# Layer A's weight sums stored ahead, one 1/rms by matmuls, and earlier splits of the second half's activations

## The chip, the cores and the metric

The kernel runs on one core of a Trainium2 chip (trn2). The metric is the time of one execution on the device in microseconds (us). A core has five engines that work side by side, each in its own order: PE (TensorE, the matmuls; PEld is its weight load), DVE (VectorE), ACT (ScalarE), POOL (GpSimd) and SP (SyncE, which here issues the DMA transfers). They wait for one another by semaphores. A DMA can also be issued on POOL's own queue.

## The reference

Two layers over x (2048 tokens of 1024), each `x <- x + mixer(RMSNorm(x))`, then a last RMSNorm. Layer A is a gated linear recurrence, layer B a short gated convolution; the width inside is 1536.

```python
def rmsnorm(x, g):
    inv = lax.rsqrt(jnp.mean(xf * xf, axis=-1, keepdims=True) + NORM_EPS)
    return xf * inv * g
def recurrent_mixer(h, ...):              # layer A
    u = einsum('bsd,dc->bsc', h, w_in)    # in-projection, 1024 -> 2 x 1536
    gate, xb = u[..., :WIDTH], u[..., WIDTH:]
    y = rg_lru(causal_depthwise_conv(xb, conv_w, conv_b), gate_w, gate_b, lam)
    return einsum('bsc,cd->bsd', y * silu(gate), w_out)   # out-projection, 1536 -> 1024
def shortconv_mixer(h, ...):              # layer B: in-projection to 4 x 1536
    return einsum('bsc,cd->bsd', bg * conv(cg * xv) * silu(gate), w_out)
```

## The kernel before

The kernel is one function, `trunk`. It works in four stages: layer A's in-projection (`in_A`, to about 646 us), layer A's out-projection (`OutSums.run`, about 646 to 868 us), layer B's in-projection and layer B's out-projection. Tokens are cut into four chunks of 512 (c = 0 to 3), two to a half. The instructions of each engine stand in an order that the framework's scheduler fixes when the kernel is built; an engine runs them strictly in that order.

**Precision.** A float32 matrix product is made of float16 parts. `split_out` (l. 1113) and `split_w` (l. 1186) make from a float32 tile a pair of float16 tiles: ACT writes the rounded value, DVE the remainder. `mm3` (l. 495) then issues three matmuls. A tile that ends up as a weight pair is called `wf`, `wv` or (on its way to DRAM) `wy`; one of the activations z is called `zs`.

**The out-projection** uses seven products instead of eight for each 2 x 2 block multiplication (Strassen and Winograd). The weights' blocks A11, A12, A21, A22 give S1 = A21 + A22, S2 = S1 - A11, S3 = A11 - A21 and S4 = A12 - S2; the activations' blocks z give T1 to T4 likewise. `ORDERS` names the seven pairs for the first half of the tokens and for the second. Each pair has four products (q = 0 to 3), so n runs from 0 to 27 in the first half and from 28 to 55 in the second. A product is 18 matmuls: KH = 6 blocks k of the inner dimension by three. After it DVE adds its result to x in `add_to_x` (l. 1300), one product late.

What a product needs is fetched and split by two lists with due times in units of n: `fetch` (SP's loads `load_z`, `load_w`, `load_raw`, `load_x`) and `splits` (`split_z`, `make_w`). The weight pairs A11, S2, S3, A22 and A12 stay in `wf` for both halves; S1 and S4 are read twice. Before the change only S1 and S4 come ready from DRAM: they were made in the in-projection by `weights` (l. 1195), a generator that loads the four raw blocks of one k, lets POOL add them (`combinations`, l. 476 to 492, the sums being l. 481), splits them and stores them. The five that stay are made in the out-projection by `make_w`: raw blocks `wo` are loaded, POOL makes S2 (two sums) and S3 (one) in l. 1233, and ACT and DVE split them (l. 1188 and 1189).

**What runs beside the in-projection.** `extra` holds generators that `advance` (l. 653) steps at each of some 188 stages of `in_A`. An entry is [counter, pace, generator]; at each stage the counter rises by one, and

```python
            if e[0] % e[1] == 0 and next(e[2], "end") == "end":
```

decides whether the generator takes a step. `weights` begins with `out_scale` (l. 810 on), which loads all 24 raw blocks and squares them on ACT (l. 816), and then goes on with the six k. Elsewhere ACT works on the recurrence in the same stretch: the gates' `tg` (tanh of the PSUM tile `pg`, l. 908), `a`, the square root of l. 926, which needs another function table (ACT_TABLE_LOAD), the squares `junk` of the next weights (l. 379) and their splits `wc` (l. 417). `pg` has two buffers, so PE's gate matmuls (l. 904) wait when ACT is late with `tg`.

**1/rms of layer A's result.** `emitA` adds the squares of each finished row block: ACT squares (l. 226), POOL adds to `sa` (l. 227). When a chunk is done, `endA` defers two steps of `inv_between` (l. 289) by so many products: the sum over partitions by four tiny matmuls (l. 233), then Sqrt on ACT (l. 245), a reciprocal on DVE (l. 246) and the spreading of the 512 values over all partitions. The spreading is done in two ways. With a queue (chunk 1 only, on POOL's): a write `rd<-r` to DRAM of 512 values of 4 bytes (l. 249) and a read back that repeats them for every partition, `inv<-rd` (l. 250). Without one: DVE makes four diagonal tiles `dg` (l. 256), PE multiplies them by ones (l. 259), ACT copies (l. 262). Chunk 1 ends before chunk 0 in the first half.

Of the kernel before, what the change touches and what calls it, by code (L numbers as in the profile page):

```python
# [11 lines left out]
ALU = mybir.AluOpType  # L12
# [20 lines left out]
KH = NH // 2  # L33
# [13 lines left out]
def trunk(ctx, tc, xT, xn, prm, wa, ga, oa, wb, ob, out):  # L47
# [18 lines left out]
    }  # L66
    wt = {
        (l, n, k): dr.tile([P, 2, CH], F16, name=f"w{l}{n}_{k}", tag=f"w{l}{n}_{k}")
        for l, names in (("A", ("S1", "S4")), ("B", ("A11", "A12", "A22", "S1", "S2", "S3", "S4")))
        for n in names  # L70
        for k in range(NH // 2)
    }
# [578 lines left out]
    extra = []  # L651
# [479 lines left out]
        "A12": ("B21", (0, 0), True),  # L1131
    }

    NZS = 18

    class OutSums:

# [9 lines left out]
        STAY = ("A11", "S2", "S3", "A22", "A12")  # L1147
        PREPARED = 2 * KH

        RAW = {"A11": (0,), "A12": (1,), "A22": (3,), "S3": (0, 2), "S2": (2, 3, 0)}  # L1150

        def __init__(self, l, wdram, wsc):
            self.l, self.wdram, self.wsc = l, wdram, wsc
# [2 lines left out]
            for half, order in enumerate(self.ORDERS):  # L1156
                seen = set()
                for p, name in enumerate(order):
                    n = 28 * half + 4 * p - (2 if l == "B" and half and p == 6 else 0)
                    for k in range(KH):  # L1160
                        at = n - 6 + 2 * k / 3
                        splits.append((at, self.split_z, half, name, k))
                        fetch.append((at - 3, self.load_z, half, name, k))
                        if half and name in self.STAY:
                            continue
                        if l == "B" or name not in self.STAY:
                            fetch.append((n - 5 + k / 100, self.load_w, half, name, k))
                            continue
                        splits.append((at + 0.1, self.make_w, name, k))
                        for r in self.RAW[name]:  # L1170
                            fetch.append((at - 2.9, self.load_raw, name, k, r))
                    dest = SEVEN[name][1]
                    if dest not in seen:
                        seen.add(dest)
                        for q in range(ND):
                            fetch.append((n + q - 3, self.load_x, half, dest, q))
# [18 lines left out]
        def weights(self, pre):  # L1195

            yield from pre
            for k in range(KH):
# [5 lines left out]
                for name, a in combinations(raw):  # L1204
                    if (self.l, name, k) in wt:
                        sp.dma_start(wt[self.l, name, k], self.split_w(wk, "wy", 2, a))
                        yield
                    if self.l == "A" and name == "S4":
                        break

        def load_z(self, half, name, k):
# [8 lines left out]
            self.wops[name, k] = t  # L1220
            return sp.dma_start(t, wt[self.l, name, k])

        def load_raw(self, name, k, n):
            t = self.raw[name, k, n] = buf(wp, "wo", "wo", 10)
            return sp.dma_start(t, self.raw_w(k, n))

        def make_w(self, name, k):
            raw = [self.raw.pop((name, k, n)) for n in self.RAW[name]]
            a = raw[0]
            for n, b in enumerate(raw[1:]):  # L1230
                t = buf(wp, "ws", "ws", 2)
                add = name == "S2" and n == 0
                g.tensor_tensor(out=t, in0=a, in1=b, op=ALU.add if add else ALU.subtract)
                a = t
            self.wops[name, k] = self.split_w(wp, "wf", 5 * KH, a)

        def load_x(self, half, dest, q):
            m, c = dest
# [196 lines left out]
            run(extra.pop(0)[2])  # L1435

    outA, startA = follows("A", oa, wsc[0])
    extra.append([-24, 3, outA.weights(preA)])
    in_A(hA, w0, head, sideA, startA, nothing)
    while sideA:  # L1440
        advance(sideA)
# [18 lines left out]
    def endA(c, ts):  # L1460
        if c == 3:
            return
        steps = inv_between(sums[c], inv[c // 2][c % 2], g if c == 1 else None)
        for n in (2, 3):
            defer(lambda: next(steps, None), n)

    def besideA(n):
# [241 lines left out]
```

## Time and profile before

| | us |
|---|---|
| median of 3 runs | 1993.2 |
| lowest, highest | 1989.6, 1994.15 |
| profiled execution, its own time | 1994.0 |
| its span, first to last instruction | 1992.2 |
| PE busy | 1943.2 (98%) |
| DVE, ACT, POOL busy | 1276.9, 1100.8, 728.0 |

The span's mean granted TensorE clock is 0.988. The profile is of one execution; a view of its trace gives start times from the span's start. In a timeline row stand start, duration, engine, line, operation, output and inputs, shape and count; what stands in brackets at its end is how long the engine was idle before it, and whose work ended that. Consecutive instructions of one kind can share a row. Matmuls overlap, so the distance of two starts, not the duration, says what one costs. The granted clock has two levels, full (2.4 GHz, 1.00) and half (1.2 GHz).

### The profile page before, as it was taken

What the parts mean: (1) busy time and instruction counts of PE and PEld (TensorE: products, weight loads), DVE (VectorE), ACT (ScalarE), POOL (GpSimd) and SP (SyncE); (2) the same over time, 40 slices, a digit from 0 to 9 for tenths busy, and PEclk for the clock granted to TensorE, in tenths of its full rate; (3) what the DMA queues carried; (4) which work ended last, traced back from release to release, by engine and by line L of the source; (5) the groups of instructions that cost most, each with busy time, mean ns of one, the idle gap of its engine ahead of it and who ended that gap; (6) DMA issues with size and microseconds to landing.
All of it is one profiled execution on the core that took longest, in us unless ns stands there. A gap on an engine that the chain in (4) does not pass through costs nothing.

```text
span 1992.2 us, 25454 instructions
## 1 busy us (share of the span) xinstructions
PE 1943.2 (98%) x8922; PEld 905.2 (45%) x8922; DVE 1276.9 (64%) x2094; ACT 1100.8 (55%) x1967; POOL 728.0 (37%) x568
## 2 busy tenths in 40 slices
PE   7999999999999998989999999999999999999998
PEld 3444444444444444444444444444444444444447
DVE  8977677767577696979635755746636336544465
ACT  7878867776667563545644443544443452544442
POOL 0012324230303360343552673664553453522321
PEclk9999999999999998999999999999999999999999
DMA  9223334220206987531241241242130030395662
GB/s 322 88 85 95 107 100 137 80 96 32 90 1 223 389 291 226 166 111 53 75 143 38 85 164 43 90 148 69 64 111 28 23 120 27 120 360 194 171 223 85
DMA packets 155617, 252.71 MB, mean 127 GB/s; under 512 B 15392, under 2 KB 52896, under 8 KB 155488
## 3 DMA queue, kind: packets, MB, share of 16 engines
q1 hardware_dynamic: 155152, 250.29, 37.3%
q8 instruction: 70, 1.15, 0.2%
q0 software_dynamic: 336, 0.79, 0.1%
q14 instruction: 59, 0.48, 0.1%
HBM read 176.04 MB, written 74.98 MB: 126 GB/s over the span
## 4 chain that ended last, share of the span: by engine, by line
PE 80%; issue 7%; DVE 6%; ACT 3%; DMA 2%; POOL 1%; DVEq 0%; POOLq 0%; ACTq 0%; SPq 0%
PE acc L497 12%; PE acc L501 12%; PE acc L500 12%; PE p L501 8%; PE p L497 8%; PE p L500 8%; PE r L497 4%; PE r L500 4%; PE r L501 4%; PE pg L904 2%; PE q L500 2%; PE q L501 2%; PE q L497 2%; DVE u L930 1%; DVE op L310 1%
## 5 line engine op out<-in xcount | busy, mean ns | idle before, releaser
L497 PEld LDWEIGHTS <-wc 128*128 128x128 f16 x2096 | 208.3, 99 | 262.4 <-issue 21.2
L500 PEld LDWEIGHTS <-wc 128*128 128x128 f16 x2096 | 205.7, 98 | 261.3 <-issue 28.0
L501 PEld LDWEIGHTS <-wc 128*128 128x128 f16 x2096 | 205.7, 98 | 260.1 <-issue 19.3
L497 PE MATMUL acc<-op,wc 128*128 128x512 f16 x752 | 285.0, 381 | 9.8 <-DVE u L871 3.3
L497 PE MATMUL p<-op,wc 128*128 128x512 f16 x768 | 291.5, 380 | 1.4 <-ACT wc L417 1.2
L500 PE MATMUL p<-op,wc 128*128 128x512 f16 x768 | 291.8, 380 | 0.0
L501 PE MATMUL p<-op,wc 128*128 128x512 f16 x768 | 291.2, 380 | 0.4 <-DVE wc L418 0.4
L500 PE MATMUL acc<-op,wc 128*128 128x512 f16 x752 | 286.8, 382 | 2.2 <-DVE op L310 2.2
L501 PE MATMUL acc<-op,wc 128*128 128x512 f16 x752 | 287.4, 382 | 0.0
L929 POOL TENSOR_TENSOR u<-fixed,u 128x512 f32<-128x512 f32 x48 | 52.2, 1109 | 361.3 <-ACT fixed L926 359.5
L418 DVE SCALAR_TENSOR_TENSOR wc<-ws,fixed,wc 128x512 f16<-128x512 f32 x104 | 105.1, 1015 | 82.1 <-ACT wc L417 72.1
L418 DVE SCALAR_TENSOR_TENSOR wc<-wr,fixed,wc 128x512 f16<-128x512 f32 x122 | 106.7, 893 | 77.7 <-ACT wc L417 72.4
L227 POOL TENSOR_TENSOR sa<-sa,sq 128x512 f32<-128x512 f32 x48 | 74.6, 1554 | 202.9 <-ACT sq L226 199.9
L1300 DVE SCALAR_TENSOR_TENSOR xo<-acc,fixed,xo 128x512 f32<-128x512 f32 (+1 forms) x120 | 84.6, 709 | 99.0 <-PE acc L501 98.6
L501 PE MATMUL r<-op,wc 128*128 128x512 f16 x384 | 145.5, 379 | 0.0
L500 PE MATMUL r<-op,wc 128*128 128x512 f16 x384 | 145.5, 379 | 0.0
L497 PE MATMUL r<-op,wc 128*128 128x512 f16 x384 | 145.5, 379 | 0.0
L993 POOL TENSOR_TENSOR pb<-pb,cg 128x512 f32<-128x512 f32 x48 | 68.8, 1433 | 187.5 <-DVE fixed L391 99.2
L862 DVE SCALAR_TENSOR_TENSOR u<-acc,fixed,u 128x511 f32<-128x511 f32 (+2 forms) x138 | 100.9, 742 | 51.5 <-ACT u L860 51.5
L417 ACT ACTIVATE wc<-wr,fixed 128x512 f16<-128x512 f32 x122 | 83.6, 711 | 78.7 <-DVE fixed L394 77.1
L904 PE MATMUL pg<-u,gts 128*128 128x512 f32 x192 | 98.7, 607 | 3.9 <-ACT tg L908 3.9
L481 POOL TENSOR_TENSOR ws<-wr 128x512 f32<-128x512 f32 x52 | 78.1, 1503 | 59.1 <-DVE wc L418 29.3
(213 smaller groups left out, 3932.8 us busy)
## 6 DMA issues: line engine op xcount, KB each, us to landing
wr<-in_wb SPq DMA_DIRECT2D x104, 256.0 KB, 3.2
zAT<-u SPq DMA_DIRECT2D x48, 256.0 KB, 2.2
zr<-zAT SPq DMA_DIRECT2D x48, 256.0 KB, 5.1
wo<-in_oa SPq DMA_DIRECT2D x48, 256.0 KB, 5.3
zr<-zBT SPq DMA_DIRECT2D x48, 256.0 KB, 5.3
wr<-in_wa SPq DMA_DIRECT2D x44, 256.0 KB, 3.8
zAB<-sg SPq DMA_DIRECT2D x36, 256.0 KB, 2.0
zr<-zAB SPq DMA_DIRECT2D x36, 256.0 KB, 5.3
```

The lines of the kernel that those rows point to most:

```text
L227: squared[0] = eng.tensor_tensor(out=acc, in0=acc, in1=sq, op=ALU.add)
L417: last_hi[0] = s.activation(t[:, 0, :], src, AF.Copy, scale=sw[:, 2:3])
L418: v.scalar_tensor_tensor(out=t[:, 1, :], in0=src, scalar=sw[:, 2:3], in1=t[:, 0, :], op0=ALU.mult, op1=ALU.subtract,)
L481: g.tensor_tensor(out=t, in0=x, in1=y, op=op)
L497: ins = nc.tensor.matmul(acc, wh, xh, start=start, stop=False, **kw)
L500: nc.tensor.matmul(acc, wh, xl, start=False, stop=False, **kw)
L501: return nc.tensor.matmul(acc, wl, xh, start=False, stop=stop, **kw)
L862: v.scalar_tensor_tensor(out=u[:, n:], in0=a[:, 0 : CH - n], scalar=ac(3 - n), in1=u[:, n:], op0=ALU.mult, op1=ALU.add,)
L904: ins = nc.tensor.matmul(pg, gw[m][:, oo], u, start=True, stop=True)
L929: g.tensor_tensor(out=u, in0=w, in1=u, op=ALU.mult)
L993: g.tensor_tensor(out=t, in0=t, in1=cg[m, half, c], op=ALU.mult)
L1300: ins = v.scalar_tensor_tensor(out=x[:, ts], in0=acc[:, ts], scalar=zsc[half][:, 2:3], in1=x[:, ts], op0=ALU.mult, op1=ALU.add,)
```

## The change

It has four parts.

1. S2 and S3 of layer A are stored in DRAM too. `weights` for A goes on to S3 in the order S1, S2, S4, S3: twelve more splits `wy`, six more sums (S3; S2 is needed for S4 already) and twelve more stores in the in-projection. In the out-projection `load_w` fetches S2 and S3 into `wf`, twelve loads in the place of thirty raw ones; `make_w` is left with A11, A12 and A22, and l. 1233 with its eighteen sums is gone. `wo` has 6 buffers instead of 10.
2. The splits of the second half's z are due at 16 + (6p + k) * 2/3 (16 to 43.3) instead of 22 + 4p + 2k/3 (22 to 49.3), their loads three earlier, with 30 buffers `zs` instead of 18.
3. The entry of `weights` in `extra` is [-60, 2] instead of [-24, 3].
4. Chunk 1's 1/rms is spread by matmuls like the others', and the second step of `inv_between` is deferred by 4 products instead of 3 for all three chunks.

```diff
-        for l, names in (("A", ("S1", "S4")), ("B", ("A11", "A12", "A22", "S1", "S2", "S3", "S4")))
+        for l, names in (("A", ("S1", "S2", "S3", "S4")), ("B", ("A11", "A12", "A22", "S1", "S2", "S3", "S4")))
...
-    NZS = 18
+    NZS = 30
...
-        RAW = {"A11": (0,), "A12": (1,), "A22": (3,), "S3": (0, 2), "S2": (2, 3, 0)}
+        RAW = {"A11": 0, "A12": 1, "A22": 3}
...
                         at = n - 6 + 2 * k / 3
+                        if l == "A" and half:
+                            at = 16 + (KH * p + k) * 2 / 3
                         splits.append((at, self.split_z, half, name, k))
                         fetch.append((at - 3, self.load_z, half, name, k))
                         if half and name in self.STAY:
                             continue
-                        if l == "B" or name not in self.STAY:
+                        if (l, name, k) in wt:
                             fetch.append((n - 5 + k / 100, self.load_w, half, name, k))
                             continue
                         splits.append((at + 0.1, self.make_w, name, k))
-                        for r in self.RAW[name]:
-                            fetch.append((at - 2.9, self.load_raw, name, k, r))
+                        fetch.append((at - 2.9, self.load_raw, name, k))
...
-                    if self.l == "A" and name == "S4":
+                    if self.l == "A" and name == "S3":
                         break
...
-        def load_raw(self, name, k, n):
-            t = self.raw[name, k, n] = buf(wp, "wo", "wo", 10)
-            return sp.dma_start(t, self.raw_w(k, n))
+        def load_raw(self, name, k):
+            t = self.raw[name, k] = buf(wp, "wo", "wo", 6)
+            return sp.dma_start(t, self.raw_w(k, self.RAW[name]))
 
         def make_w(self, name, k):
-            raw = [self.raw.pop((name, k, n)) for n in self.RAW[name]]
-            a = raw[0]
-            for n, b in enumerate(raw[1:]):
-                t = buf(wp, "ws", "ws", 2)
-                add = name == "S2" and n == 0
-                g.tensor_tensor(out=t, in0=a, in1=b, op=ALU.add if add else ALU.subtract)
-                a = t
-            self.wops[name, k] = self.split_w(wp, "wf", 5 * KH, a)
+            self.wops[name, k] = self.split_w(wp, "wf", 5 * KH, self.raw.pop((name, k)))
...
-    extra.append([-24, 3, outA.weights(preA)])
+    extra.append([-60, 2, outA.weights(preA)])
...
-        steps = inv_between(sums[c], inv[c // 2][c % 2], g if c == 1 else None)
-        for n in (2, 3):
+        steps = inv_between(sums[c], inv[c // 2][c % 2])
+        for n in (2, 4):
             defer(lambda: next(steps, None), n)
```

POOL at the end of the first half, before (`ws<-wo` are the sums of l. 1233, `sa` the squares of the chunks):

```order
L1233 TENSOR_TENSOR ws<-wo 128x512 x5
L227 TENSOR_TENSOR sa<-sa,sq 128x512
L1233 TENSOR_TENSOR ws<-wo 128x512
L227 TENSOR_TENSOR sa<-sa,sq 128x512 x8
L249 DMA rd<-r 128x4x1
L250 DMA inv<-rd 128x512
L227 TENSOR_TENSOR sa<-sa,sq 128x512 x5
L481 TENSOR_TENSOR ws<-wr 128x512
```

POOL at the same place, with the change:

```order
L764 TENSOR_TENSOR u<-sg,u 128x512
L227 TENSOR_TENSOR sa<-sa,sq 128x512 x17
L481 TENSOR_TENSOR ws<-wr 128x512
L481 TENSOR_TENSOR ws<-ws,wr 128x512
L227 TENSOR_TENSOR sa<-sa,sq 128x512 x2
```

The sums and the two DMAs have left the queue, and the squares stand in one run.

ACT in the in-projection, the stretch that the trace of before shows from 212.60 us on (the square root, the splits `wc` of the next weights, the two `tg` of a gate), before:

```order
L926 ACT_TABLE_LOAD
L926 ACTIVATE fixed<-fixed 128x1024
L417 ACTIVATE wc<-wr,fixed 128x512 x4
L908 ACT_TABLE_LOAD
L908 ACTIVATE tg_2012<-pg,fixed 128x512
L379 ACTIVATE junk,fixed<-wr 128x512 x2
L908 ACTIVATE tg_2016<-pg,fixed 128x512
```

ACT at the same place, with the change:

```order
L926 ACT_TABLE_LOAD
L926 ACTIVATE fixed<-fixed 128x1024
L1189 ACTIVATE wy<-ws,fixed 128x512 x2
L379 ACTIVATE junk,fixed<-wr 128x512
L417 ACTIVATE wc<-wr,fixed 128x512 x4
L1189 ACTIVATE wy<-ws,fixed 128x512
L908 ACT_TABLE_LOAD
L908 ACTIVATE tg_2056<-pg,fixed 128x512
L1189 ACTIVATE wy<-ws,fixed 128x512
L908 ACTIVATE tg_2060<-pg,fixed 128x512
```

Three splits `wy` and one `junk` now stand between the square root and the first `tg`. (In the changed file the ACT half of `split_w` is l. 1189.)

## Rows read from the trace of the kernel before

**Rows 1.** The page: engines, busy us (share of the span), instructions.

```profile
PE 1943.2 (98%) x8922; PEld 905.2 (45%) x8922; DVE 1276.9 (64%) x2094; ACT 1100.8 (55%) x1967; POOL 728.0 (37%) x568
```

**Rows 2.** Windows: stretch, its length, busy us of each engine, PEclk, DMA share, GB/s.

```profile
50.00:240.00 190.00, 178.35 (x734) 80.14 (x734) 142.90 (x273) 157.73 (x281) 35.78 (x28) 0.96 0.29 94
240.00:640.00 400.00, 398.20 (x1731) 181.19 (x1730) 278.21 (x513) 275.65 (x440) 109.74 (x83) 1.00 0.27 90
755.00:768.00 13.00, 6.75 (x20) 3.50 (x21) 3.85 (x6) 2.89 (x4) 3.09 (x3) 0.62 0.82 240
748.00:760.00 12.00, 6.86 (x32) 2.94 (x30) 0.33 (x1) 0.63 (x1) 1.90 (x3) 0.92 0.37 29
1871.00:1881.00 10.00, 10.00 (x48) 4.55 (x47) 4.90 (x7) 0.34 (x1) 0.00 (x0) 1.00 1.06 143
```

**Rows 3.** Timeline of POOL, the small write and the read behind it.

```profile
745.74 0.92 POOL L249 DMA_DIRECT2D rd<-r  x1
758.01 0.56 POOL L250 DMA_DIRECT2D inv<-rd  x1 [11.35 <-DMA rd<-r]
```

**Rows 4.** Timeline of PE behind that, L233 and the first matmuls.

```profile
761.25 1.87 PE L233 MATMUL ss<-fixed,sa 128*128 128x1 f32 x8 [6.39 <-POOL sa L227]
762.98 0.59 PE L497 MATMUL acc<-zs,wf 128*128 128x512 f16 x1
...
768.38 0.38 PE L500 MATMUL acc<-zs,wf 128*128 128x512 f16 x1
```

**Rows 5.** Timeline of PE near 713 us.

```profile
713.18 0.38 PE L497 MATMUL acc<-zs,wf 128*128 128x512 f16 x1 [2.47 <-DVE xo L1300]
...
713.99 0.63 PE L497 MATMUL acc<-zs,wf 128*128 128x512 f16 x1
...
717.24 0.38 PE L501 MATMUL acc<-zs,wf 128*128 128x512 f16 x1
```

**Rows 6.** Source view of lines 1188 and 1189: ns of one, min/median/max.

```profile
L1188 ACT ACTIVATE wy<-ws,fixed x36: 705/712/724, 285.3 to 1430.7; 128x512 f16<-128x512 f32 x36
...
L1189 DVE SCALAR_TENSOR_TENSOR wf<-ws,fixed,wf x12: 739/1374/1755, 681.5 to 720.7; 128x512 f16<-128x512 f32 x12
```

**Rows 7.** Timeline of PE near 857 us, the 1/rms of chunk 2.

```profile
853.39 0.38 PE L497 MATMUL acc<-zs,wv 128*128 128x512 f16 x1
857.63 0.79 PE L259 MATMUL pn<-dg,fixed 128*128 128x128 f32 x2 [3.87 <-DVE dg L256]
...
861.09 0.63 PE L500 MATMUL acc<-zs,wv 128*128 128x512 f16 x1
...
863.97 0.38 PE L501 MATMUL acc<-zs,wv 128*128 128x512 f16 x1
```

**Rows 8.** Timeline of DVE: product 49's add, dg of chunks 2 and 0.

```profile
854.77 0.74 DVE L1300 SCALAR_TENSOR_TENSOR xo<-acc,fixed,xo 128x512 f32<-128x512 f32 x1
...
856.57 3.65 DVE L256 TENSOR_SCALAR dg<-fixed,r 128x128 f32<-128x128 f32 x4
...
769.82 0.87 DVE L256 TENSOR_SCALAR dg<-fixed,r 128x128 f32<-128x128 f32 x4
```

**Rows 9.** Groups by line, 640 to 755 us: count, busy us, mean ns, idle.

```profile
L1116 DVE SCALAR_TENSOR_TENSOR zs<-zr,fixed,zs 128x512 f16<-128x512 f32 x43 | 43.5, 1021 | 5.3 <-ACT zs L1115 5.1
...
L1189 DVE SCALAR_TENSOR_TENSOR wf<-ws,fixed,wf 128x512 f16<-128x512 f32 x12 | 15.0, 1253 | 3.9 <-ACT wf L1188 3.9
...
L1233 POOL TENSOR_TENSOR ws<-wo 128x512 f32<-128x512 f32 x12 | 18.4, 1543 | 37.3 <-DMA wo<-in_oa 35.2 <-DVE wf L1189 1.9 <-POOL ws L1233 0.2
```

**Rows 10.** Timeline of PE, waits in the in-projection.

```profile
125.75 0.38 PE L497 MATMUL acc<-op,wc 128*128 128x512 f16 x1 [3.33 <-DVE u L871]
...
219.45 2.07 PE L904 MATMUL pg<-u,gts 128*128 128x512 f32 x2 [3.94 <-ACT tg L908]
```

**Rows 11.** Timeline of ACT before that tg.

```profile
214.85 2.54 ACT L417 ACTIVATE wc<-wr,fixed 128x512 f16<-128x512 f32 x4
```

**Rows 12.** Source view of line 249, its three writes.

```profile
DMA to landing us min/median/max: 10.8/11.7/12.0
```

## The prediction

> **What bounds the kernel now.** I read the page first: PE is busy for 1943.2 of 1992.2 us [rows 1]. The 49 us in which it idles, and what it loses at half clock, are all that this change can win, since it removes no product. The windows view says where they lie [rows 2]: from 240 to 640 us PE is busy for 398.20 of 400.00, so nothing is to be had there; from 50 to 240 us, in layer A's in-projection, for 178.35 of 190.00; from 755 to 768 us, in its out-projection, for 6.75 of 13.00 at a clock of 0.62. About 0.2% (4 us) is what a measurement of this kernel can tell from no change.
>
> In the out-projection I then read the timelines, and three waits stand out. **Near 755 us** POOL issues the small write `rd<-r` at 745.74, and its queue stands 11.35 us until the write has landed and `inv<-rd` may go [rows 3]. Chunk 0's squares, which POOL has to add, are queued behind it, and PE's L233 waits for those: 6.39 us idle, then half clock [rows 4], with thirteen matmul starts from 762.98 to 768.38. **At 713 us** PE waits 2.47 us for DVE's add L1300 and then runs at half clock, eight starts from 713.99 to 717.24 [rows 5]. DVE is late there since it splits S2, S3 and z beside POOL's sums L1233: one such split takes between 0.74 and 1.76 us [rows 6]. **At 857 us** the matmuls L259 of chunk 2 wait 3.87 us for DVE's `dg`, and half clock follows till 863.97 [rows 7]. Behind it stands DVE's queue: product 49's add ran at 854.77 [rows 8], though PE had done with that product some 845 us in (two products of 18 matmuls and an L233 back from 853.39); the Sqrt of chunk 2 is behind that add's square in ACT's order; and the four `dg` then took 3.65 us, where chunk 0's took 0.87 [rows 8].
>
> **The change, part by part.** The sum is made against the profiled execution's own time, 1994.0 us; the median of the three runs, 1993.2, is 0.8 lower. Where PE ran at half clock, 1.2 instead of 2.4 GHz, half of the time is counted as lost.
>
> **A, 1/rms of chunk 1 by matmuls.** `rd<-r` and `inv<-rd` leave POOL's queue, and chunk 0's squares (17 in a row now) have nothing before them. Gone are 6.39 us idle, half of L233's 1.87, and half of the 5.40 us of thirteen starts [rows 4]: 6.4 + 0.9 + 2.7 = 10.0. New on PE are four L259 matmuls: a pair of them took 0.79 us at half clock [rows 7], so four some 0.8 at full clock. DVE's four `dg` and the ACT copy lie beside other work. A is **-9.2**. The new L259 stand two products behind their L233 in PE's order and can wait there as chunk 2's do: nothing if DVE keeps up, 8.1 (below, under C) if it doesn't. I take **+1**, near the low end, since chunk 0's `dg`, the nearest in time, took 0.87 us [rows 8].
>
> **B, S2 and S3 from DRAM.** From 640 to 755 us twelve splits `wf<-ws` go (15.0 us of DVE) and eighteen sums L1233, twelve of which are 18.4 us of POOL [rows 9]. Nine more z splits of the second half come in: by their due times 19 instead of 10 are done by product 28. At 1021 ns [rows 9] that is 9 us, so DVE has 6 us less to do, and without POOL beside it its operations go to the lower end of rows 6. The wait at 713 goes: 2.47, and half of the 3.25 us of eight starts [rows 5], 1.6. B is **-4.1** (bounds 0, if the z splits refill DVE just there, and -4.1). Twelve loads of S2 and S3 on SP's queue replace thirty raw blocks of the same 256 KB; in SP's order they wait on nothing but early products. I cost them at nothing, covered by the products up to n = 16; without that cover PE would wait at the first S2 product for one such load.
>
> **C, fewer z splits in the second half.** The same nine are missing after product 28; the last is due at 43.3 instead of 49.3. At 0.74 to 1.76 us each [rows 6] 6.7 to 15.8 us of DVE leave, where product 49's add is some 10 us late. From 853.39 to 861.09 [rows 7] are 7.7 us, of which 0.2 is the usual distance and 0.8 the L259's own: 6.7. Half of 861.09 to 863.97 is 1.4. At most -8.1. I take **-6**: Sqrt still stands behind chunk 3's squares in ACT's order, so a part may stay. Bounds 0 and -8.1.
>
> **D, the in-projection.** Twelve more splits and six more sums come here, with twelve stores on SP. The counter of -60 delays nothing (its remainder by 2 is 0, as that of -24 by 3 was): the generator runs every second step instead of every third, so its 24 squares, and then the splits, come earlier and closer. One split costs ACT 0.712 us, DVE 0.74 to 1.76 [rows 6]: 8.5 us of ACT and about 12 of DVE in all, covered by PE's products. The cover is thin before 240 us, where ACT is busy for 157.73 of 190.00, and good behind it (275.65 of 400.00) [rows 2]. One place is concrete. At 219.45 PE waits 3.94 us for ACT's `tg` [rows 10]; ACT had four `wc` splits, 2.54 us, ahead of it [rows 11]. In the new order three `wy` splits and a `junk` stand there too, four operations of about 0.71: 2.8 us more. I take **+4**: these, and one more place of the kind with about 1. Bounds: +12 (three more waits like 219.45's) and -4 (squares that are out of the way sooner free the wait at 125.75, 3.33, with its half clock [rows 10]).
> The Trainium skill, SBUF — State Buffer, section Who interferes with whom, says that a DVE instruction with two SBUF inputs contends with a GpSimd one that reads SBUF and blocks where it issues second. The traces agree [rows 6], and an estimate by it is that six sums at 1.5 us [rows 9] could hold DVE 9 us longer; if all of it reached PE, D would be +13 and the sum -5.3.
>
> Sum: -9.2 + 1 - 4.1 - 6 + 4 = -14.3, so 1979.7 by the profiled execution and 1978.9 by the median. I forecast **1979**.
>
> **The rivals.**
> *Slower: the in-projection pays more than the out-projection wins.* PE meets ACT late at each of the weights' six steps (four raw blocks, their sums, their splits), where splits, `wc` and table loads stand ahead of a `tg`. At 219.45's 3.94 us each that is +23.6. Less A, B and C it is +5.3 if C comes as forecast and +11.3 if it doesn't: 1998.5 to 2004.5. It decides from D = +18 on, five such waits. For it: ACT's 83% before 240 us. Against it: behind 240 us PE idled less than 2 us in 400 while the twelve S1 and S4 splits were made there. Chance 0.08.
> *No difference that shows: chunk 1's new L259 wait as chunk 2's did, and chunk 2's stay.* -9.2 + 8.1 - 4.1 + 0 + 4 = -1.2: 1992. For it: DVE is what is late at 713 and at 857, and both chains end on DVE. Against it: the 0.87 us at 769.82. Chance 0.10.
> *The wait at 857 stays, the rest goes as forecast.* -9.2 + 1 - 4.1 + 4 = -8.3: 1985. It needs the Sqrt to stand for product 49's square as before. Chance 0.17.
> *The small write isn't what slows the transfers.* From 748 to 760 us all queues together moved 29 GB/s; but from 1871 to 1881, with another `rd<-r` under way, 143 [rows 2], and that write landed no sooner: 10.8 to 12.0 us at all three places [rows 12]. If the slow stretch near 755 comes from something else, ACT's z splits stand for their loads there as before, chunk 0's squares with them, and A gives nothing: +1 - 4.1 - 6 + 4 = -5.1, 1988. Chance 0.06.
> The Trainium skill, DMA: Bandwidth & Descriptors, section Anatomy of one DMA — SWDGE (gpsimd) path, speaks for this rival: it gives such a DMA a fixed 2.0 us and its bytes over 436 GB/s, an estimate of 2 us for these 2 KB, so that what made it 10.8 or more would lie elsewhere. The trace's time for it differs from the page's.
> *D is nil or a gain, down to -4.* -18.3 to -22.3: 1971 to 1975. Chance 0.07.
>
> **How the numbers follow.** The forecast's own case, 1975 to 1984, has 0.52. Over 0.2% faster is below 1989.2: 0.52 + 0.17 + 0.06 + 0.07 = 0.82, of which 0.01 goes to the case within 0.2%, as 1988 lies near its edge: 0.81. Within 0.2%: 0.10 + 0.01 = 0.11. Slower: 0.08. The range from 1970 to 1991 takes in the gains and the near edge of no difference; it leaves out the slower case and most of the 0.10, some 0.17.
>
> **What the profile of the changed kernel would show.** A: no `rd<-r` in the out-projection, no wait of POOL for a DMA there, no wait of PE over 1 us at chunk 0's L233, clock 1.00 from 755 to 768 us. B: no wait of PE for L1300 near product 15, DVE less busy from 640 to 755 us. C: product 49's add right behind its product, chunk 2's L259 with no wait over 1 us. D: the wait for `tg` near 219 us at 6 to 7 us, and at most one new one. Wrong it is if PE's idle time between 50 and 640 us grows by over 12 us, or if chunk 1's L259 wait for several us.

## The result, and the profile after

The changed kernel takes 1979.05 us (median of 5 runs, 1975.62 to 1983.94) against 1992.6 us of the kernel before (5 runs, 1989.51 to 1994.15, three of them those of the table ahead and two new). The ratio is 0.9938, 95% interval 0.9919 to 0.9957: 0.6% faster. Its profiled execution took 1978.52 us, with a span of 1976.7.

The row of the page that answers to [rows 1]: PE is busy for 6.8 us less than before and idle for 40.3 us instead of 49.0.

```profile
PE 1936.4 (98%) x8930; PEld 904.1 (46%) x8930; DVE 1278.6 (65%) x2098; ACT 1099.9 (56%) x1968; POOL 707.6 (36%) x554
```

The windows view of the changed kernel, with the columns of [rows 2]:

```profile
50.00:240.00 190.00, 181.21 (x777) 82.27 (x775) 156.78 (x294) 162.60 (x290) 45.76 (x34) 0.99 0.35 115
240.00:640.00 400.00, 390.94 (x1683) 176.82 (x1681) 280.79 (x512) 280.56 (x449) 108.73 (x83) 0.99 0.26 89
640.00:755.00 115.00, 115.00 (x551) 54.25 (x550) 86.29 (x130) 66.38 (x115) 26.31 (x18) 1.00 0.93 337
755.00:768.00 13.00, 13.00 (x66) 6.48 (x65) 8.86 (x18) 5.31 (x10) 0.00 (x0) 1.00 0.80 266
...
748.00:760.00 12.00, 12.00 (x62) 5.98 (x60) 5.85 (x12) 3.76 (x6) 0.23 (x1) 1.00 0.84 276
```

The place near 755 us is gone: 13.00 of 13.00 at full clock, where [rows 2] have 6.75 at 0.62; the stretch from 748 to 760 moves 276 GB/s instead of 29. From 640 to 755 us PE now runs without a gap. From 50 to 240 us PE is busy for 181.21 instead of 178.35, but from 240 to 640 for 390.94 instead of 398.20: a new loss, most of it in one wait, 6.49 us at 252.77 (below).

To set the two traces side by side, each is cut at five matmuls: the scale of the second weights (l. 388), the first matmul of product 0, those of products 28 and 32, and the last of product 55. Timeline of PE, kernel before:

```profile
44.30 0.28 PE L388 MATMUL pt<-fixed 128*128 128x4 f32 x2
...
632.44 0.38 PE L497 MATMUL acc<-zs,wv 128*128 128x512 f16 x1
...
746.93 0.38 PE L497 MATMUL acc<-zs,wf 128*128 128x512 f16 x1
...
774.24 0.38 PE L497 MATMUL acc<-zs,wf 128*128 128x512 f16 x1
...
877.56 0.38 PE L501 MATMUL acc<-zs,wv 128*128 128x512 f16 x1
```

and the changed kernel:

```profile
47.58 0.28 PE L388 MATMUL pt<-fixed 128*128 128x4 f32 x2
...
634.83 0.38 PE L497 MATMUL acc<-zs,wv 128*128 128x512 f16 x1
...
745.72 0.38 PE L497 MATMUL acc<-zs,wf 128*128 128x512 f16 x1
...
762.96 0.38 PE L497 MATMUL acc<-zs,wf 128*128 128x512 f16 x1
...
865.20 0.38 PE L501 MATMUL acc<-zs,wv 128*128 128x512 f16 x1
```

| stretch | before, us | after, us | difference |
|---|---|---|---|
| start to the second scale | 44.3 | 47.6 | +3.3 |
| in-projection, to product 0 | 588.1 | 587.2 | -0.9 |
| products 0 to 27 | 114.5 | 110.9 | -3.6 |
| products 28 to 31 | 27.3 | 17.2 | -10.1 |
| products 32 to 55 | 103.3 | 102.2 | -1.1 |
| rest, to the span's end | 1114.6 | 1111.5 | -3.1 |

The first row is not the change's: PE ran its first 26 us partly at half clock in this execution. Of the twelve kernels below, later_rms2 shows the second scale at 43.5 us and idle_write at 47.4, with the same instructions.

PE's waits of more than 2.5 us behind the first 60 us of the changed kernel, and the L259 of chunks 1 and 2 (timeline of PE). One more, 2.21 us at 334.29, answers to one of 1.80 at 341.61 before.

```profile
129.28 0.38 PE L497 MATMUL acc<-op,wc 128*128 128x512 f16 x1 [3.59 <-DVE u L871]
...
252.77 0.59 PE L497 MATMUL acc<-op,wc 128*128 128x512 f16 x1 [6.49 <-DVE sg L956]
...
744.83 1.05 PE L259 MATMUL pn<-dg,fixed 128*128 128x128 f32 x8
...
837.69 1.87 PE L233 MATMUL ss<-fixed,sa 128*128 128x1 f32 x8 [2.99 <-POOL sa L227]
...
848.99 1.05 PE L259 MATMUL pn<-dg,fixed 128*128 128x128 f32 x8
```

The L259 of chunk 1 (744.83), the four new matmuls (each stands as two instructions, so x8), take 0.89 us to the next start and wait for nothing, and so does that of chunk 2 (848.99), where [rows 7] have 3.87 us. But chunk 2's L233, one step ahead of it, now waits 2.99 us and is followed by half clock. The waits of [rows 4, 5] have gone. In the in-projection the wait at 219.45 of [rows 10] has gone too, and a longer one stands at 252.77.

### The profile page after: what moved, and what is told of

It is laid out like the page before. It is cut to its first block, busy times and chain, and to the rows that moved or that the text cites. A ratio compares the mean times of both kernels' runs of the same rounds, so it can differ in the third digit from the quotient of the medians.

```text
span 1976.7 us, 25501 instructions
## 1 busy us (share of the span) xinstructions
PE 1936.4 (98%) x8930; PEld 904.1 (46%) x8930; DVE 1278.6 (65%) x2098; ACT 1099.9 (56%) x1968; POOL 707.6 (36%) x554
## 4 chain that ended last, share of the span: by engine, by line
PE 79%; DVE 3%; DMA 0%; ACT 0%; issue 0%; POOL 0%; SPq 0%; DVEq 0%; ACTq 0%; POOLq 0%
PE acc L497 11%; PE acc L500 11%; PE acc L501 11%; PE p L501 8%; PE p L497 8%; PE p L500 8%; PE r L497 4%; PE r L500 4%; PE r L501 4%; PE pg L904 2%; PE q L500 2%; PE q L501 2%; PE q L497 2%; DVE op L310 1%; PE ss L233 0%; DMA wr<-in_wb 0%
## 5 line engine op out<-in xcount | busy, mean ns | idle before, releaser
L862 DVE SCALAR_TENSOR_TENSOR u<-acc,fixed,u 128x511 f32<-128x511 f32 (+2 forms) x138 | 100.8, 741 | 43.5 <-ACT u L860 43.5
L379 ACT ACTIVATE junk<-wr 128x512 f32<-128x512 f32 x136 | 84.3, 621 | 31.8 <-DMA wr<-in_wa 16.1
L930 DVE TENSOR_TENSOR_SCAN u<-a,fixed,u 128x512 f32<-128x512 f32 x48 | 78.5, 1638 | 35.4 <-POOL u L929 35.4
```

Source lines behind the costliest of these rows:

```text
L379: ins = s.activation(junk, t, AF.Square, accum_out=sq[:, m : m + 1])
L862: v.scalar_tensor_tensor(out=u[:, n:], in0=a[:, 0 : CH - n], scalar=ac(3 - n), in1=u[:, n:], op0=ALU.mult, op1=ALU.add,)
L930: v.tensor_tensor_scan(out=u, data0=a, data1=u, initial=stA[:, h : h + 1], op0=ALU.mult, op1=ALU.add,)
```

## The experiments

The twelve runs, with the stretches cut as above, in us, each from its own trace. The ratio is to the kernel before, timed again beside each group; that kernel's own median moved between 1991.5 and 1994.4 us, so ratios compare better than medians. A stretch stands for one execution: the half clock behind one and the same wait differs between executions by 2 us and more (last section).

| kernel | median | ratio, interval | in-projection | 0 to 27 | 28 to 31 | 32 to 55 |
|---|---|---|---|---|---|---|
| before | 1992.6 | | 588.1 | 114.5 | 27.3 | 103.3 |
| the change | 1979.05 | 0.9938 (0.9919 to 0.9957) | 587.2 | 110.9 | 17.2 | 102.2 |
| rms_only | 1982.95 | 0.9951 (0.9936 to 0.9966) | 590.0 | 115.3 | 17.2 | 104.1 |
| rms_by_dma | 1976.9 | 0.9920 (0.9905 to 0.9935) | 589.1 | 110.0 | 17.6 | 100.7 |
| idle_write | 1977.9 | 0.9927 (0.9912 to 0.9941) | 590.0 | 110.9 | 17.2 | 100.3 |
| raw_sums | 1980.26 | 0.9936 (0.9919 to 0.9952) | 586.5 | 115.7 | 18.1 | 101.8 |
| old_due | 1980.63 | 0.9934 (0.9919 to 0.9949) | 589.3 | 110.9 | 17.2 | 103.1 |
| old_pace | 1973.66 | 0.9902 (0.9885 to 0.9918) | 586.1 | 110.9 | 17.2 | 99.9 |
| true_delay | 1967.14 | 0.9868 (0.9853 to 0.9882) | 578.9 | 110.9 | 17.2 | 100.0 |
| later_rms2 | 1978.78 | 0.9929 (0.9914 to 0.9943) | 591.2 | 110.9 | 17.2 | 96.9 |
| raw_by_dma | 1985.16 | 0.9964 (0.9951 to 0.9977) | 585.9 | 114.5 | 22.0 | 103.3 |
| due_by_dma | 1980.87 | 0.9940 (0.9917 to 0.9963) | 590.0 | 110.0 | 18.5 | 103.0 |
| delay_by_dma | 1968.02 | 0.9875 (0.9857 to 0.9894) | 578.2 | 110.0 | 17.3 | 102.1 |
| delay_later_rms2 | 1970.4 | 0.9885 (0.9864 to 0.9905) | 579.6 | 110.9 | 17.2 | 97.5 |

### Part 4 alone

In the kernel before, only `endA` is changed:

```diff
-        steps = inv_between(sums[c], inv[c // 2][c % 2], g if c == 1 else None)
-        for n in (2, 3):
+        steps = inv_between(sums[c], inv[c // 2][c % 2])
+        for n in (2, 4):
```

> The kernel before with part 4 alone (chunk 1's 1/rms by matmuls, second steps deferred by 4). My account (the small write holds POOL's queue and slows all transfers): about 8 us faster than before, 1984 to 1986; chunk 0's L233 waits under 1 us, all queues move well over 100 GB/s in the 12 us behind chunk 1's Sqrt, ACT waits for no z load over 5 us there; the waits near 713 and 857 stay. Rival (the write doesn't slow the transfers): ACT still stands over 10 us for a z load, L233 still waits some 6 us, time within 3 us of before.

Measured: 1982.95 us, 8.7 below the 1991.66 of the kernel before beside it. Products 28 to 31 take 17.2 us instead of 27.3, and chunk 0's L233 waits for nothing. The other two waits are where they were (timeline of PE):

```profile
714.16 0.49 PE L497 MATMUL acc<-zs,wf 128*128 128x512 f16 x1 [2.27 <-DVE xo L1300]
...
849.17 0.49 PE L259 MATMUL pn<-dg,fixed 128*128 128x128 f32 x2 [3.50 <-DVE dg L256]
```

ACT's longest wait for a z load there is 3.79 us, where before it was 13.83. In the kernel before, part 4 gains what step A said. (Its second deferral, 4 products instead of 3, was not run alone. It can't touch a chunk spread by the small write, since `inv_between` yields between its steps only without a queue.)

### The small write back in the changed kernel

```diff
-        steps = inv_between(sums[c], inv[c // 2][c % 2])
+        steps = inv_between(sums[c], inv[c // 2][c % 2], g if c == 1 else None)
```

> The changed kernel with chunk 1's 1/rms spread by the small write and read on POOL's queue again. My account: some 8 us slower than the changed kernel, 1986 to 1989; L233 of chunk 0 waits 5 to 8 us behind POOL, PE at half clock after it. Rival (with the sums gone from POOL and z split earlier the write is hidden): within 3 us of the changed kernel.

Measured: 1976.9 us. The rival's result: the changed kernel loses nothing by it. Timeline of POOL and, last, of PE in this run:

```profile
737.90 0.92 POOL L249 DMA_DIRECT2D rd<-r  x1
747.86 0.56 POOL L250 DMA_DIRECT2D inv<-rd  x1 [9.04 <-PE acc L501]
748.44 2.62 POOL L227 TENSOR_TENSOR sa<-sa,sq 128x512 f32<-128x512 f32 x2
...
751.11 1.05 PE L233 MATMUL ss<-fixed,sa 128*128 128x1 f32 x8
```

The write still holds POOL's queue, for 9.04 us (the view puts that wait down to another releaser; it ends as the write lands). But chunk 0's squares end at 748.44 + 2.62 = 751.06, and PE's L233 for them starts at 751.11, with no wait. The write was issued 3.35 us behind chunk 1's L233 here, and 7.5 us behind it before. The reason is ACT's Sqrt. Chunk 1's L233 and the Sqrt behind it, kernel before:

```profile
738.25 1.05 PE L233 MATMUL ss<-fixed,sa 128*128 128x1 f32 x8
...
743.26 0.26 ACT L245 ACTIVATE r<-ss,fixed 128x4 f32<-128x4 f32 x1
```

and rms_by_dma:

```profile
734.55 0.95 PE L233 MATMUL ss<-fixed,sa 128*128 128x1 f32 x8
...
735.53 0.26 ACT L245 ACTIVATE r<-ss,fixed 128x4 f32<-128x4 f32 x1 [0.67 <-PE ss L233]
```

In the kernel before, the Sqrt stands behind z splits and a square that waits for DVE, and comes 5.0 us after L233; here 1.0. The numbers close: from chunk 1's L233 to the write are 7.49 us before and 3.35 here, 4.1 less; from the write to the read behind it 12.27 (745.74 to 758.01) and 9.96 (737.90 to 747.86), 2.3 less. Together that is 6.4, the whole wait of 6.39. So the wait near 755 us was made by two things, a small write that took some 10 to 12 us to the read, and DVE being late; rms_only, without the write, and this run, without the lateness, have none. Here the squares had 0.05 us to spare, so that there is none at all is also luck.

### Which part makes DVE late there

`raw_by_dma` undoes part 1 as well (`RAW`, `load_raw`, `make_w` as in the kernel before, `wt` without S2 and S3, `weights` ending at S4); `due_by_dma` undoes part 2 as well (`NZS = 18`, the two lines with the new due times taken out).

> The changed kernel with parts 1 and 4 undone together for chunk 1 (S2 and S3 made in the out-projection, 1/rms by the small write and read), parts 2 and 3 kept. Why did the small write cost nothing in rms_by_dma, where before it cost 6.4 us and half clock? Theory: it has some 16 us from chunk 1's L233 to chunk 0's, takes about 10, and before lost 5 to 7 of them to ACT and DVE being late with splits. With the raw sums back, Sqrt comes 3 us or more behind L233 and chunk 0's L233 waits 3 to 8 us: 5 to 9 us slower than raw_sums, 1985 to 1989. Rival (only the z splits' due times matter for it): no wait, within 3 us of raw_sums.

> The changed kernel with parts 2 and 4 undone together for chunk 1 (old due times of z, 1/rms by the small write and read), S2 and S3 from DRAM. Theory as for raw_by_dma, by the raw sums: Sqrt within 2 us of L233, no wait over 1 us at chunk 0's L233, within 3 us of old_due. Rival (the z splits' due times decide): a wait of 3 to 8 us there, 1985 to 1989.

Measured: 1985.16 us for the first, 4.9 above raw_sums; 1980.87 for the second, as old_due. With the raw sums back chunk 1's Sqrt comes 4.7 us after L233 again, and PE waits 4.17 us in products 28 to 31, with half clock behind it. The place is not the one expected: three squares now stand ahead of `inv<-rd` in POOL's order, so chunk 0's L233 is in time; but ACT stands 9.33 us for a z load that was issued beside the write, with chunk 0's Sqrt behind it, and L259 is late (timelines of PE and ACT):

```profile
742.23 0.95 PE L233 MATMUL ss<-fixed,sa 128*128 128x1 f32 x8
...
746.91 0.26 ACT L245 ACTIVATE r<-ss,fixed 128x4 f32<-128x4 f32 x1
...
763.53 0.72 ACT L1115 ACTIVATE zs<-zr,fixed 128x512 f16<-128x512 f32 x1 [9.33 <-DMA zr<-zAT]
...
767.12 0.25 ACT L245 ACTIVATE r<-ss,fixed 128x4 f32<-128x4 f32 x1
...
768.47 1.47 PE L259 MATMUL pn<-dg,fixed 128*128 128x128 f32 x8 [4.17 <-DVE dg L256]
```

With the old due times the Sqrt comes 1.0 us behind (738.65 after 737.67), and L233 waits 0.98 us. So it is part 1's work in the out-projection (sums, splits and raw loads of S2 and S3, which were not taken apart) that made DVE and ACT late, not the due times of the z splits; and a late write costs PE by POOL's queue in one order and by ACT's in another.

### Part 1 undone alone

As in raw_by_dma, with 1/rms by matmuls kept.

> The changed kernel with part 1 undone: S2 and S3 are made in the out-projection from raw blocks (18 POOL sums and 12 more splits there, 12 fewer in the in-projection), z still split earlier. My account (DVE's load and POOL's sums made the wait at 713): waits of PE for DVE's add L1300 between 640 and 755 us of 2 to 8 us in all, each with half clock behind it, 4 to 10 us slower there; the in-projection 1 to 3 us different. Time 1983 to 1989. Rival (the wait at 713 was one unlucky order): no wait over 1 us there, within 2 us of the changed kernel.

Measured: 1980.26 us, not to be told from the changed kernel. Products 0 to 27 lose what was expected, 4.8 us (timeline of PE):

```profile
712.54 0.38 PE L497 MATMUL acc<-zs,wf 128*128 128x512 f16 x1 [1.67 <-DVE xo L1302]
...
722.49 0.82 PE L501 MATMUL acc<-zs,wf 128*128 128x512 f16 x3 [2.01 <-DVE wf L1191]
```

but the in-projection, with twelve splits fewer, is at 586.5 us against 587.2 to 591.2 in the six kernels that share the changed kernel's in-projection (mean 589.5). Of the waits expected, one for the add came, 1.67 us with full clock behind it; the other, 2.01 us for a split `wf`, has half clock behind it. The time expected, 1983 to 1989, was missed, since the other side gives 3 us back.

### A small write that nobody waits for

In the changed kernel `inv_from` writes `rd<-r` on POOL's queue for chunk 1, as before, and reads nothing back:

```diff
+        if probe:
+            rd = dr.tile([CH], F32, tag="rd", name="rd", bufs=2)
+            g.dma_start(rd.rearrange("(i p) -> p i", p=P), r)
         pn = ps.tile([P, CH], F32, tag="g", name="pn", bufs=2)[:, 0 : n * P]
```

> The changed kernel with the same small write (512 values of 4 bytes, POOL's queue) issued at the same place, but nobody waits for it: no read back, 1/rms still by matmuls. If the write itself slows the transfers: the queues fall from 276 GB/s to under 100 for some 10 us behind it, z loads land late, but with 1/rms free of it the time is within 3 us of the changed kernel. If it does not slow them: the rate stays at 200 GB/s or more and the write lands in under 5 or in 10 to 12 us all the same, time equal too. The windows tell the two apart, not the time.

Measured: 1977.9 us, within the 3 us. The write landed 10.9 us after its issue at 742.18. In the ten us from 742.60 on the queues moved 54 GB/s, against 90 in the same stretch of the changed kernel, which has no write (740.00 to 750.00): SP's queue stands in both for stores of x that wait for DVE, so the rates settle little here. The transfers one by one do. The store of x issued at 744.50, with the write under way, against those of the changed kernel without it; DMA issues, median us to landing in the last column, this run from 744 to 746 us:

```profile
x<-xo SPq DMA_DIRECT2D x1, 256.0 KB, 9.6
```

the changed kernel, from 745 to 756:

```profile
xo<-in_xT SPq DMA_DIRECT2D x6, 256.0 KB, 5.1
x<-xo SPq DMA_DIRECT2D x1, 256.0 KB, 2.0
```

and rms_by_dma from 740 to 744.2, eight transfers, all issued while its write (737.90 to 747.30) was under way:

```profile
zr<-zAT SPq DMA_DIRECT2D x4, 256.0 KB, 10.2
xo<-in_xT SPq DMA_DIRECT2D x3, 256.0 KB, 9.5
x<-xo SPq DMA_DIRECT2D x1, 256.0 KB, 9.6
```

None of the eight landed before the write did; the first came 2.6 us behind it. Windows view of that run, seven us up to the write's landing and seven behind it (DMA share and GB/s are the last two numbers):

```profile
740.30:747.30 7.00, 7.00 (x34) 3.21 (x33) 1.30 (x2) 1.19 (x2) 0.00 (x0) 1.00 1.01 89
747.30:754.30 7.00, 6.95 (x37) 3.48 (x36) 2.40 (x4) 2.17 (x3) 3.10 (x3) 1.00 0.84 268
```

With the write under way the DMA engines are busy all the time and move a third of what they move behind it. The same holds in every trace: of the 87 transfers that SP issued while such a write was under way, and whose landing the traces tell, none landed before the write, among them the seven of the kernel before that were issued from 1870.29 on beside the write of [rows 2] at 143 GB/s. So the first reading holds: the write does not stop the bytes, but it holds back what is issued beside it until it has landed itself.

### Part 2 undone

`NZS = 18` and the old due times, in the changed kernel.

> The changed kernel with part 2 undone (z of the second half due at 22 to 49.3, 18 buffers). My account (those splits made DVE late near chunk 2's 1/rms): the 3.0 us wait at L233 turns into more, in all 3 to 8 us of PE idle between 820 and 866 us with half clock behind it; 2 to 6 us slower than the changed kernel, 1981 to 1985. Rival (the wait there is made by DVE's work for layer B's input and by where L233 stands, not by z splits): within 2 us of the changed kernel, the same wait of about 3 us.

Measured: 1980.63 us, with an interval that covers the changed kernel's ratio. Chunk 2's wait goes back to where it was (timeline of PE):

```profile
846.39 0.80 PE L259 MATMUL pn<-dg,fixed 128*128 128x128 f32 x2 [3.83 <-DVE dg L256]
```

Products 32 to 55 take 103.1 us, 102.2 with the change. In the four traces that have the change's instructions there (the change, idle_write, old_pace, true_delay) they take 99.9 to 102.2, on the mean 100.6; in all four the wait is 2.98 or 2.99 us, and only the half clock behind it differs. Part 2 moved a wait by one step and gained 1 to 3 us; the times of the two kernels do not tell them apart.

### The pace, and a delay that acts

`old_pace` has `extra.append([-24, 3, outA.weights(preA)])` again. `true_delay` holds the generator for 30 of its steps, which at pace 2 are 60 stages:

```diff
-    extra.append([-60, 2, outA.weights(preA)])
+    def held(gen):
+        for _ in range(30):
+            yield
+        yield from gen
+    extra.append([0, 2, held(outA.weights(preA))])
```

> The changed kernel with part 3 undone (weights stepped every third stage, counter -24). If the faster pace costs (my forecast of +4 for the in-projection): PE's waits from 60 to 640 us are smaller, no wait of 6.5 us near 253, 2 to 6 us faster than the changed kernel. If it wins, as the trace of the changed kernel hints (its waits at 183 and 219 us are gone): PE waits 3 us or more near 183 and near 219 again, 0 to 5 us slower.

> The changed kernel with a delay that acts: the weights' generator starts 60 stages later, pace 2 as in the change. The squares then run from about a third of the in-projection on and the splits behind them, some 240 us later than in the changed kernel. My account (thin ACT and DVE cover before 260 us makes the 6.5 us wait at 253): that wait goes, with its half clock, 5 to 8 us faster, 1971 to 1974, if no new wait comes with the later splits. Rival (the waits there are between the gates and the conv alone): waits of 2 to 4 us near 125, 183 or 219 as before, within 2 us.

Measured: 1973.66 us for the old pace, 1967.14 for the delay, 0.9902 and 0.9868 of before. The faster pace costs the change some 5 us by the medians; the two intervals only just do not touch. Of the 5.8 us between the two profiled executions some 1 lies in the in-projection (3.4 against the mean of the six), 2.4 in the start and 2.3 in products 32 to 55, so the traces show only a part of this cost where the pace acts. With the old pace the waits of the kernel before are back and the one at 252.77 is gone (timeline of PE):

```profile
183.01 0.54 PE L497 MATMUL acc<-op,wc 128*128 128x512 f16 x1 [2.34 <-DVE fixed L866]
...
219.82 1.30 PE L904 MATMUL pg<-u,gts 128*128 128x512 f32 x2 [4.13 <-ACT tg L908]
```

With the delay, the waits that remain in the in-projection are smaller, and it takes 578.9 us, 8 to 12 less than with the instructions of before or of the change: more than the 5 to 8 us that were expected, since the wait at 129.28 shrinks too. Chunk 2's L233 still waits 2.99 us (timeline of PE):

```profile
125.31 0.38 PE L497 MATMUL acc<-op,wc 128*128 128x512 f16 x1 [1.72 <-DVE fixed L866]
...
182.87 1.42 PE L904 MATMUL pg<-u,gts 128*128 128x512 f32 x2 [2.65 <-ACT tg L908]
```

What made the wait at 252.77 shows in the changed kernel's timeline of ACT:

```profile
245.46 0.72 ACT L1189 ACTIVATE wy<-ws,fixed 128x512 f16<-128x512 f32 x1 [3.25 <-POOL ws L481]
247.59 0.72 ACT L1189 ACTIVATE wy<-ws,fixed 128x512 f16<-128x512 f32 x1 [1.41 <-POOL ws L481]
...
251.31 1.27 ACT L955 ACTIVATE sg<-acc,fixed 128x512 f32<-128x512 f32 x2
```

ACT stands 3.25 and 1.41 us for POOL's sums of the weights, with the `sg` of the gate behind them in its queue; DVE's `sg` and PE wait for that. The weights' steps are there because the generator runs at pace 2 from the first stage on: with the old pace and with the delay the wait is gone, while raw_sums, at pace 2 without the twelve splits, still has 5.00 us there, at 252.40.

### Chunk 2's 1/rms one product later

```diff
-        for n in (2, 4):
+        for n in ((3, 5) if c == 2 else (2, 4)):
...
-        if n >= 52:
-            for kk in range(2 * n - 104, 2 * n - 102):
+        if n >= 53:
+            for kk in range(3 * n - 159, min(KB, 3 * n - 156)):
```

> The changed kernel with chunk 2's 1/rms one product later (steps deferred by 3 and 5 instead of 2 and 4; the normalisation of the last chunks spread over three products instead of four to make room). If the 3.0 us wait at chunk 2's L233 is only a matter of its place in PE's order: the wait goes with its half clock, 4 to 6 us faster, 1973 to 1975. If DVE's work for layer B is late by more than a product: a wait of 2 to 4 us at L233 or L259 stays, within 2 us.

Measured: 1978.78 us, no difference. The wait went, and a longer one came 78 us later (timeline of PE):

```profile
837.43 0.97 PE L233 MATMUL ss<-fixed,sa 128*128 128x1 f32 x8
...
915.40 0.61 PE L497 MATMUL p<-op,wc 128*128 128x512 f16 x1 [4.35 <-ACT wc L417]
```

Products 32 to 55 take 96.9 us, 5.3 less; the rest to the span's end takes 1976.4 - 859.6 = 1116.8, 5.3 more. The wait at 915.40 is for ACT's first `wc` split of layer B's second unit, whose scale stands in DVE's queue behind the work on layer B's input. In the changed kernel the same place waits 1.23 us (917.85): here the `wc` comes 2.5 us earlier, but PE has done with product 55 5.6 us earlier (859.6 against 865.2), so 3.1 us go into the longer wait, and half clock to about 920 takes most of the rest. (The edit also moves the normalisation of the last chunks; no run shows which of the two sets the `wc`.) What makes chunk 2's L233 wait is, by the order of the queues, the same work; no run takes it away. Timeline of DVE in the changed kernel:

```profile
832.17 2.36 DVE L310 TENSOR_TENSOR op<-t,op 128x512 f16<-128x512 f32 x2
834.45 0.74 DVE L1294 SCALAR_TENSOR_TENSOR xo<-acc,fixed,xo 128x512 f32<-128x512 f32 x1
```

and of POOL:

```profile
836.00 1.64 POOL L227 TENSOR_TENSOR sa<-sa,sq 128x512 f32<-128x512 f32 x1 [2.02 <-ACT sq L226]
```

The last add of chunk 2 stands behind splits `op` of layer B's input (1.2 us each beside POOL's sums), its square follows at 835.23 and the sum at 836.00; L233 starts at 837.69, when that is done.

### Both together

`delay_by_dma` is true_delay with the small write, `delay_later_rms2` is true_delay with chunk 2's step one product later.

> true_delay (weights' generator held for 60 stages) with chunk 1's 1/rms by the small write and read. If part 4 is worth nothing once ACT and DVE are on time: within 2 us of true_delay's 1967.1. If the 0.05 us that the squares had to spare in rms_by_dma were luck: a wait of 1 to 4 us at chunk 0's L233 and half clock, 1969 to 1974.

> true_delay with chunk 2's 1/rms one product later, as in later_rms2. There the 3.0 us wait at L233 went and one of 4.35 us came back at the first products of layer B's second unit, behind DVE's queue. If DVE's work for layer B sets the end there whatever PE does: the same exchange, within 2 us of true_delay. If the later weights leave DVE freer: 3 to 5 us faster, 1962 to 1964.

Measured: 1968.02 and 1970.4 us. The small write costs nothing that shows in the best version either. The later step wins 2.5 us in products 32 to 55 and loses 6.1 behind them, at a wait of 5.12 us before that same `wc`; the time is 3.3 us above true_delay, outside the 2 us expected, with intervals that overlap. true_delay, at 1967.14, has the lowest median of the study, 12 us below the change; delay_by_dma is not to be told from it.

## Why the prediction was right

The forecast was 1979 us and the time is 1979.05; the sum was -14.3, the profiled executions differ by 15.5. That close a fit is partly luck: C came 3 to 5 us short and D 3.5 to 5 us cheaper than forecast, so that two errors cancel; and the start (+3.3) and the rest (-3.1), which the sum does not have, cancel too.

**A (-9.2, and +1 for a new wait)** was right in size. Products 28 to 31 lost 10.1 us, and the new L259 wait for nothing. (The step read the x2 of [rows 7] as two of the four matmuls; it is one. That cost nothing: the four take 0.89 us, against its 0.8.) Alone, part 4 gains 8.7. What the step had wrong is the cause: it named the write alone. rms_by_dma and raw_by_dma show that the wait also needed a Sqrt that came 5 us late, which part 1 cures: 4.1 of the 6.4 us are that, 2.3 the write's longer way to the read. A and B were added as if they were independent; for this wait they are two cures for one illness, and with part 1 in place part 4 measures as nothing. The total hid this, since the wait goes once either way. The rival "the small write isn't what slows the transfers" falls: no transfer issued beside it landed before it, those of its own example from 1871 us on included, and part 4 alone did take the wait away. The 2 us that an estimate by the Trainium skill's page DMA: Bandwidth & Descriptors, section Anatomy of one DMA — SWDGE (gpsimd) path, gave for such a write are not what the runs show: none landed in under 7.5 us.

**B (-4.1)** was right: products 0 to 27 lost 3.6 us, with the new L259 (0.9 at most) inside. raw_sums brings back 4.8, with the waits for DVE's add and split. Its loads cost nothing, as was said.

**C (-6)** is the first step that failed: products 32 to 55 lost 1.1 us in the profiled execution, some 3 by the mean of the four traces, so most of the wait stayed, in another place. The sign named for C, no wait of chunk 2's L259, came all the same. The step took the z splits for DVE's backlog there. old_due shows that they mainly decide at which of the two steps, L233 or L259, PE waits; the backlog is, by the order of DVE's queue, the work on layer B's input. Even without the wait no time was won, as later_rms2 shows: PE then waits for the same queue behind 910 us. The rival "the wait at 857 stays, the rest goes as forecast" described this place better than the forecast did.

**D (+4)** is the second. In the profiled execution the in-projection lost 0.9 us, and over the six kernels with the same instructions there (587.2, 589.1, 590.0, 589.3, 591.2, 590.0) its mean is 589.5, against 588.1 and 590.0 with the instructions of before. So it is about nil, and the 0.9 contains some 1.7 of chance: the wait near 126 us has half clock behind it before, and none in the changed kernel. The rival "D is nil or a gain" described this step. The concrete place was named wrongly: the four operations did come ahead of the `tg` at 219 us, but no wait of PE stands there any more, and those of 183.56 (2.28) and 219.45 (3.94) are gone with their half clock. In their place came one of 6.49 us at 252.77, by the mechanism that the step had (ACT in order, the weights' splits ahead of the gate's work), through `sg` and POOL's sums. With the old pace the in-projection takes 586.1 us, 3.4 less than that mean, and the kernel 5 us less. But without the twelve splits, at the new pace, it takes 586.5 and 585.9 (raw_sums, raw_by_dma): either half of D alone lies 3 us below both together, and 1.6 to 4 below the order of before, so they are no costs that add up. This rests on one or two traces each. That the -60 delays nothing was right; a delay that acts is worth 12 us in the time, 8 to 11 of them seen in the in-projection.

**Not foreseen:** the rest of the span lost 3.1 us. Half of that is a half-clock stretch before, 932.4 to 935.4, behind waits of 1.20 and 0.42 us that the changed kernel has too (1.23 and 0.43), without half clock. rms_only, with the order of before, has none there either, so it comes and goes with the execution. Another 0.9 is the small write again, in layer B's out-projection: before, POOL's `inv<-rd` stands there 11.76 us for a write that landed after 12.0, and the L233 behind it, at 1883.45, waits 0.61; in the changed kernel, with the same instructions, the write landed after 9.5 and L233 waits for nothing. The start's +3.3 weighs against it.

## What to carry to other kernels

Two cures for one wait must not be added: ask, for each wait, which chain ends last and whether a second part of the change shortens the same chain. A wait that vanishes at one place has gained nothing until the next place where the same late engine is waited for has been checked; here 5.3 us were won by 860 us and lost again behind 915, to a longer wait and the half clock behind it. And a counter that is tested by its remainder alone does not delay: where a side task is meant to start late, look in the order at where its first instruction stands.

## What was not expected of the hardware

A wait of the same length is not always followed by half clock. The wait near 129 us for DVE's `u` is 3.59 us in the changed kernel, with full clock behind it; in idle_write it is 3.58, with half clock from 129.4 to 134.6. Eleven of the fourteen traces have this wait, 3.27 to 3.60 us long; seven show half clock behind it and four (the change, old_pace, later_rms2, raw_by_dma) none. A term that books half clock behind every wait is thus an upper bound for that place.

The start differs by up to 4 us between executions of the same instructions: the second scale stands at 43.5 us in later_rms2 and at 47.6 in the changed kernel, where L233 and the eight matmuls behind it ran at half clock from 18.25 us on. Differences of 3 us between two single traces mean nothing unless they are cut by stage.

A write of 512 values of 4 bytes took 7.5 to 12.0 us to land wherever the traces tell its landing, whether the queues were full or quiet, and no transfer issued on SP's queue while it was under way landed before it: 256 KB loads took 9 to 11 us beside it in rms_by_dma, 15 to 16 in the kernel before, and 4 to 6 without it in the changed kernel; a store that takes 2.0 us took 9.6.
